# Attention scores on one core: whole head pairs on 128 columns, 16 KB output runs and two-bank transposed tiles

## The chip, the cores and the metric

The kernel runs on one core of a Trainium2 chip. The metric is the device time of one execution in microseconds (us). Engines are called as in the profile: PE is TensorE (matmuls and transposes), DVE is VectorE, ACT is ScalarE, POOL is GpSimd, SP is SyncE, which issues all DMAs here.

## The reference

```
q, k : (8, 8, 512, 64) float32        # batch, heads, sequence, head dimension
scale = 1 / sqrt(64)
out[b, h] = scale * q[b, h] @ k[b, h].T        # (8, 8, 512, 512) float32
```

The inputs are 16.78 MB together and the output is 67.11 MB.

## The kernel before

The work is cut into four units (`v`) of two batches each, and each unit into four output tiles (`t`) of 4 MB: sixteen stores in all. There are five steps.

**Loads and casts** (`load_and_cast`, lines 78 and 82). At the start SP issues, for each unit, one 2 MB load of k and one of q; each of the 128 partitions takes a run of 16 KB. The float32 data of a unit fill one buffer of the pool `big`. POOL casts them to bf16 (`xb`), four casts per unit. `big` has three buffers, which the output tiles use too, so the load of the fourth unit waits for the casts of the first, and an output tile waits until the data that were in its buffer have been cast or stored.

**Transposes** (`transpose`, lines 107 and 116). PE transposes 128x128 blocks of k and q against an identity into a PSUM tile `tp` of eight blocks, one bank. The pool of `tp` has two buffers. A unit has eight such tiles, four for k and four for q.

**Copies** (`rearrange`, line 95). Four copies bring each `tp` to SBUF in another order: to `kT`, or to `qz`, which keeps zeros in the half of its partitions that belongs to the other batch. DVE and ACT take whole tiles in turn (`n_tp % 2`).

**Scores and evacuations** (`scores`, lines 126, 66 and 64). An output tile consists of eight PSUM tiles `ps` of two banks, from a pool of three buffers. Each is filled by four matmuls of 64 columns by 512, two heads on the two column halves, and then scaled and written to the output tile `o` by DVE or ACT: of every six, ACT takes numbers 0, 2 and 3. A partition of `o` holds 16 rows of the output of one head, 32 KB in a row.

**Stores** (line 141). When the eight evacuations are done, SP issues one DMA of 4 MB.

The order of the work is that of the program, held on each engine by `pinned`. The transposes of unit v+1 are a generator, `ahead`, of which `take` draws some steps after each evacuation of unit v. One step is either all transposes of one `tp` or one copy. The first unit is transposed ahead of everything. In unit 0 two steps are drawn per evacuation from the second output tile on:

```
for n, _ in enumerate(scores(v, t)):
    take(ahead, 1 + (n % 4 == 3) if v else 2 * (t > 0))
```

Of the kernel before, what the change touches and what calls it, by code (L numbers as in the profile page):

```python
# [1 line left out]

# [5 lines left out]


@with_exitstack  # L10
def kernel(
    ctx: ExitStack,
    tc: tile.TileContext,
    q: bass.AP,
    k: bass.AP,
    out: bass.AP,
):

    nc = tc.nc
    B, H, S, D = q.shape
    scale = 1.0 / (D ** 0.5)
    P = 128
    UNITS = B // 2
    N = H
    M = P // (2 * H)  # L30
    R = S // M
    J = R // 2
    RO = 16
    U = S // RO
    JJ = J // RO
    IW = 8 // JJ
    TILES = N // 2

    f32 = mybir.dt.float32
    bf16 = mybir.dt.bfloat16  # L40

    q_r = q.rearrange("(v b) g (m j) d -> v (b g m) (j d)", b=2, j=R)
    k_r = k.rearrange("(v b) g (m j) d -> v (b g m) (j d)", b=2, j=R)
    out_r = out.rearrange("(v b) (t h) (u i) k -> v (b t) (h u) (i k)", b=2, h=4, i=RO)

    consts = ctx.enter_context(tc.tile_pool(name="consts", bufs=1))

    big_pool = ctx.enter_context(tc.tile_pool(name="big", bufs=3))
    bf_pool = ctx.enter_context(tc.tile_pool(name="bf", bufs=6))
    t_pool = ctx.enter_context(tc.tile_pool(name="t", bufs=2))  # L50
    tpsum_pool = ctx.enter_context(tc.tile_pool(name="tpsum", bufs=2, space=bass.MemoryType.PSUM))
    psum_pool = ctx.enter_context(tc.tile_pool(name="psum", bufs=3, space=bass.MemoryType.PSUM))


    pinned = tc.keep_in_program_order

    n_evac = 0
    n_tp = 0

    def evacuate(dst, src):  # L60
        nonlocal n_evac

        if n_evac % 6 in (0, 2, 3):
            pinned(nc.scalar.mul(out=dst, in_=src, mul=scale))  # L64
        else:
            pinned(nc.vector.tensor_scalar(out=dst, in0=src, scalar1=scale, scalar2=None,  # L66
                                           op0=mybir.AluOpType.mult))
        n_evac += 1

    def half(h):  # L70
        return slice(h * D, (h + 1) * D)

    def load_and_cast(v):

        xf = big_pool.tile([P, 2, 2, J * D], f32, name="big")
        both = []
        for x, src in enumerate((k_r, q_r)):
            nc.sync.dma_start(out=xf[:, x], in_=src[v].rearrange("p (s c) -> p s c", s=2))
        for x in range(2):
            xb = bf_pool.tile([P, J, 2, D], bf16, name="xb")  # L80
            for s in range(2):
                pinned(nc.gpsimd.tensor_copy(out=xb[:, :, s, :],  # L82
                                             in_=xf[:, x, s].rearrange("p (j d) -> p j d", j=J)))
            both.append(xb)
        return both

    def rearrange(tp, pattern, dst):

        nonlocal n_tp
        copy = (nc.vector.tensor_copy, nc.scalar.copy)[n_tp % 2]  # L90
        n_tp += 1
        for s in range(2):
            src = tp[half(s)].rearrange(pattern, n=N, h=2)
            for h in range(2):
                pinned(copy(out=dst(s, h), in_=src[:, h]))  # L95
                yield

    def transpose(v, kb, qb):


        kT = t_pool.tile([P, N, M, 2, J], bf16, name="kT")
        qz = qzs[v % 2]
        ts[v] = (kT, qz)
        for j0 in range(0, J, 8):
            tp = tpsum_pool.tile([P, 8, P], bf16, name="tp")
            for j in range(8):
                pinned(nc.tensor.transpose(out=tp[:, j, :], identity=identity,  # L107
                                           in_=kb[:, j0 + j].rearrange("p s d -> p (s d)")))
            yield
            yield from rearrange(tp, "d j (n h m) -> d h n m j",  # L110
                                 lambda s, h: kT[half(h), :, :, s, j0:j0 + 8])
        for i0 in range(0, RO, IW):
            tp = tpsum_pool.tile([P, IW, JJ, P], bf16, name="tp")
            for i in range(IW):
                for jj in range(JJ):
                    pinned(nc.tensor.transpose(out=tp[:, i, jj, :], identity=identity,  # L116
                                               in_=qb[:, RO * jj + i0 + i].rearrange("p s d -> p (s d)")))
            yield
            yield from rearrange(tp, "d i jj (n h m) -> d h i n m jj",
                                 lambda s, h: qz[half(h), i0:i0 + IW, :, h * U:(h + 1) * U]  # L120
                                 .rearrange("d i n (m s jj) -> d s i n m jj", s=2, jj=JJ)[:, s])

    def matmul(v, t, i, x, dst):

        kT, qz = ts[v]
        pinned(nc.tensor.matmul(out=dst, lhsT=qz[:, i, 2 * t + x, :],  # L126
                                rhs=kT[:, 2 * t + x].rearrange("d m s j -> d (m s j)"),
                                start=True, stop=True))

    def scores(v, t):  # L130

        o = big_pool.tile([P, RO, S], f32, name="big")
        for i in range(0, RO, 2):
            ps = psum_pool.tile([P, 2, S], f32, name="ps")
            for w in range(2):
                for x in range(2):
                    matmul(v, t, i + w, x, ps[half(x), w, :])
            evacuate(o[:, i:i + 2, :], ps)
            yield
        src = o.rearrange("p i k -> p (i k)")  # L140
        nc.sync.dma_start(out=out_r[v, t], in_=src)  # L141

    def take(steps, count):
        for _ in range(count):
            next(steps, None)

    identity = consts.tile([P, P], dtype=bf16)
    make_identity(nc, identity)
    qzs = [consts.tile([P, RO, N, 2 * U], bf16, name=f"qz{n}") for n in range(2)]
    for qz in qzs:  # L150
        nc.vector.memset(qz, 0.0)  # L151
    cast = [load_and_cast(v) for v in range(UNITS)]

    ts = {}
    for _ in transpose(0, *cast[0]):
        pass
    for v in range(UNITS):
        ahead = transpose(v + 1, *cast[v + 1]) if v + 1 < UNITS else iter(())
        for t in range(TILES):

            for n, _ in enumerate(scores(v, t)):
                take(ahead, 1 + (n % 4 == 3) if v else 2 * (t > 0))
        for _ in ahead:
            pass


# [1 line left out]
_INS = ['q', 'k']  # L168
_OUTS = [((8, 8, 512, 512), 'float32')]


# [23 lines left out]
```

## Time and profile before

| | |
|---|---|
| median of three runs | 203.78 us (203.74 to 204.09) |
| the profiled execution, whole | 203.86 us |
| its span, first to last instruction | 202.1 us |
| PE busy | 107.7 us, 53% of the span |
| DVE busy | 126.4 us, 63% |
| ACT busy | 101.1 us, 50% |
| POOL busy | 30.5 us, 15% |
| DMA: data moved, mean rate | 84.00 MB, 416 GB/s |
| mean granted PE clock | 0.833 |

A line of the groups gives the line of the kernel, the engine, the operation, output and input with their shapes and the count; then the busy time and the mean of one in ns; then the idle time of the engine just before, with what ended it. A line of the timeline gives start and duration in us. The slices cut the span in 40 equal parts: the DMA digit is the busy share of the 16 DMA engines in tenths, 9 meaning 90% or more.

### The profile page before, as it was taken

The page shows a single profiled execution, that of the slowest core. Times are in us where ns is not written, and L with a number is a line of the kernel's source. Part 1 is how long each engine was busy: PE and PEld are TensorE (multiplying, and loading weights), DVE is VectorE, ACT ScalarE, POOL GpSimd, SP SyncE. Part 2 cuts the span into 40 slices and gives each one's busy share as a digit, 9 for nine tenths or more (in the row PEclk, how much of TensorE's full clock was granted, in tenths as well). Part 3 has the DMA queues.
Part 4 walks back from the last instruction along what each step waited for, and adds up shares of the span by engine and source line. Part 5 has one row for each costly group of instructions (what it writes and reads, how often), then busy time and mean ns, then how long its engine had stood idle before and what let it go on. Part 6 is the DMA issues. An engine that isn't in the chain of part 4 may idle for free.

```text
span 202.1 us, 1976 instructions
## 1 busy us (share of the span) xinstructions
PE 107.7 (53%) x768; PEld 55.7 (28%) x768; DVE 126.4 (63%) x130; ACT 101.1 (50%) x129; POOL 30.5 (15%) x22
## 2 busy tenths in 40 slices
PE   0033488663784767765858685856765366710000
PEld 0033344332342333332423332322322133400000
DVE  6736677974987689997569797479457064530000
ACT  2016665793639586974857566746526241520000
POOL 1277777655000000000000000000000000000000
PEclk9999999998769999997878888888589957555555
DMA  6999999999999999999999999999999999999991
GB/s 214 428 444 415 435 441 422 418 412 428 454 438 417 441 417 428 438 448 435 422 415 425 448 435 448 415 418 428 435 448 441 415 428 438 441 428 441 415 415 58
DMA packets 3464, 84.00 MB, mean 416 GB/s; under 512 B 384, under 2 KB 384, under 8 KB 384
## 3 DMA queue, kind: packets, MB, share of 16 engines
q1 hardware_dynamic: 3456, 83.89, 97.2%
q8 instruction: 6, 0.10, 0.2%
q14 instruction: 2, 0.02, 0.0%
HBM read 16.78 MB, written 67.11 MB: 415 GB/s over the span
## 4 chain that ended last, share of the span: by engine, by line
DMA 33%; DVE 14%; PE 6%; ACT 2%; issue 1%; DVEq 0%; ACTq 0%; SPq 0%
DMA out_dram<-big 33%; DVE big L66 9%; PE ps L126 6%; DVE kT L95 3%; ACT big L64 2%; DVE qz L95 1%; ACT kT L95 1%; PE tp L107 0%; DVEq L66 0%; ACTq L64 0%; SPq L141 0%
## 5 line engine op out<-in xcount | busy, mean ns | idle before, releaser
L126 PE MATMUL ps<-kT,qz 128*64 128x512 bf16 x512 | 85.0, 456 | 47.2 <-ACT big L64 36.6
L66 DVE TENSOR_SCALAR big<-ps 128x1024 f32<-128x1024 f32 x64 | 76.2, 1221 | 38.9 <-DMA out_dram<-big 25.0
L64 ACT ACTIVATE big<-ps 128x1024 f32<-128x1024 f32 x64 | 63.9, 1023 | 56.9 <-DMA out_dram<-big 24.5
L126 PEld LDWEIGHTS <-qz 128*64 128x64 bf16 x512 | 35.6, 124 | 85.9 <-issue 75.7
L82 POOL CAST xb<-big 128x2048 bf16<-128x2048 f32 x16 | 29.8, 1893 | 17.1 <-DMA big<-in_k_dram 9.6
L95 DVE COPY kT<-tp 64x512 bf16<-64x512 bf16 x32 | 22.0, 687 | 7.3 <-PE tp L107 6.9
L95 ACT COPY kT<-tp 64x512 bf16<-64x512 bf16 x32 | 18.5, 578 | 15.2 <-PE tp L107 14.9
L95 DVE COPY qz<-tp 64x512 bf16<-64x512 bf16 x32 | 22.0, 688 | 3.9 <-PE tp L116 3.3
L95 ACT COPY qz<-tp 64x512 bf16<-64x512 bf16 x32 | 18.5, 578 | 4.0 <-PE tp L116 3.6
L107 PE MATMUL tp<-identity,xb 128*128 128x128 bf16 x128 | 12.0, 253 | 15.0 <-POOL xb L82 12.4
L116 PE MATMUL tp<-identity,xb 128*128 128x128 bf16 x128 | 13.3, 272 | 7.8 <-ACT qz L95 4.1
L107 PEld LDWEIGHTS <-xb 128*128 128x128 bf16 x128 | 9.5, 114 | 20.8 <-POOL xb L82 12.4
L116 PEld LDWEIGHTS <-xb 128*128 128x128 bf16 x128 | 10.6, 123 | 14.4 <-issue 14.1
L151 DVE MEMSET qz<- 128x4096 uint32 x2 | 6.9, 3472 | 2.5 <-PEq L179 1.7
L95 ACT ACT_TABLE_LOAD x1 | 1.3, 1283 | 0.7 <-PEq L179 0.7
masks.py:199 POOL TENSOR_SCALAR_AFFINE_SELECT identity<-identity 128x128 bf16<-128x128 bf16 x1 | 0.3, 292 | 0.1
masks.py:197 POOL MEMSET identity<- 128x128 bf16 x1 | 0.2, 204 | 0.3 <-POOLq L179 0.3
L179 POOL MEMSET const-float32-0.0<- 128x1 f32 x1 | 0.1, 98 | 0.2 <-issue 0.2
L179 POOL MEMSET const-bfloat16-1.0<- 128x1 bf16 x1 | 0.1, 101 | 0.0
L179 POOL MEMSET const-uint8-127<- 128x1 uint8 x1 | 0.1, 101 | 0.0
L179 POOL MEMSET const-float32-1.0<- 128x1 f32 x1 | 0.1, 98 | 0.0
## 6 DMA issues: line engine op xcount, KB each, us to landing
out_dram<-big SPq DMA_DIRECT2D x16, 4096.0 KB, 21.2
big<-in_k_dram SPq DMA_DIRECT2D x4, 2048.0 KB, 18.9
big<-in_q_dram SPq DMA_DIRECT2D x4, 2048.0 KB, 23.9
```

The lines of the kernel that those rows point to most:

```text
L64: pinned(nc.scalar.mul(out=dst, in_=src, mul=scale))
L66: pinned(nc.vector.tensor_scalar(out=dst, in0=src, scalar1=scale, scalar2=None, op0=mybir.AluOpType.mult))
L82: pinned(nc.gpsimd.tensor_copy(out=xb[:, :, s, :], in_=xf[:, x, s].rearrange("p (j d) -> p j d", j=J)))
L95: pinned(copy(out=dst(s, h), in_=src[:, h]))
L107: pinned(nc.tensor.transpose(out=tp[:, j, :], identity=identity, in_=kb[:, j0 + j].rearrange("p s d -> p (s d)")))
L116: pinned(nc.tensor.transpose(out=tp[:, i, jj, :], identity=identity, in_=qb[:, RO * jj + i0 + i].rearrange("p s d -> p (s d)")))
L126: pinned(nc.tensor.matmul(out=dst, lhsT=qz[:, i, 2 * t + x, :], rhs=kT[:, 2 * t + x].rearrange("d m s j -> d (m s j)"), start=True, stop=T ...
L151: nc.vector.memset(qz, 0.0)
L179: nc = _bacc.Bacc("TRN2", target_bir_lowering=False, num_devices=1)
```

## The change

The head pair `x` moves from the column halves of a matmul to the free dimension of the output tile. A matmul now has 128 columns for one pair of heads, and a `ps` tile takes two matmuls. A partition of `o` holds 8 rows of each of two heads' outputs, two runs of 16 KB that lie 2 MB apart in the output; a store is still 4 MB. A transposed tile has 16 blocks and two banks, and a copy twice the elements; a unit has four such tiles and 16 copies. The pool of `tp` has one buffer, where it had two. The first unit's transposed tiles take their buffers from the pool of `ps` instead. In unit 0 the steps of `ahead` are drawn in the third and fourth output tile alone, one per evacuation and two after every fourth; in later units they are drawn after evacuations 0, 1, 3, 5 and 7, which is one transposed tile with its four copies for each output tile.

```diff
-    RO = 16
+    RO = 8
...
-    IW = 8 // JJ
+    IW = 16 // JJ
...
-    out_r = out.rearrange("(v b) (t h) (u i) k -> v (b t) (h u) (i k)", b=2, h=4, i=RO)
+    out_r = out.rearrange("(v b) (t x h) (u i) k -> v (b t) (h u) x (i k)", b=2, x=2, h=2, i=RO)
...
-    tpsum_pool = ctx.enter_context(tc.tile_pool(name="tpsum", bufs=2, space=bass.MemoryType.PSUM))
+    tpsum_pool = ctx.enter_context(tc.tile_pool(name="tpsum", bufs=1, space=bass.MemoryType.PSUM))
...
-        for j0 in range(0, J, 8):
-            tp = tpsum_pool.tile([P, 8, P], bf16, name="tp")
-            for j in range(8):
+        pool, name = (tpsum_pool, "tp") if v else (psum_pool, "ps")
+        for j0 in range(0, J, 16):
+            tp = pool.tile([P, 16, P], bf16, name=name)
+            for j in range(16):
...
-                                 lambda s, h: kT[half(h), :, :, s, j0:j0 + 8])
+                                 lambda s, h: kT[half(h), :, :, s, j0:j0 + 16])
         for i0 in range(0, RO, IW):
-            tp = tpsum_pool.tile([P, IW, JJ, P], bf16, name="tp")
+            tp = pool.tile([P, IW, JJ, P], bf16, name=name)
...
-    def matmul(v, t, i, x, dst):
+    def scores(v, t):
         kT, qz = ts[v]
-        pinned(nc.tensor.matmul(out=dst, lhsT=qz[:, i, 2 * t + x, :],
-                                rhs=kT[:, 2 * t + x].rearrange("d m s j -> d (m s j)"),
-                                start=True, stop=True))
-    def scores(v, t):
-        o = big_pool.tile([P, RO, S], f32, name="big")
-        for i in range(0, RO, 2):
-            ps = psum_pool.tile([P, 2, S], f32, name="ps")
-            for w in range(2):
-                for x in range(2):
-                    matmul(v, t, i + w, x, ps[half(x), w, :])
-            evacuate(o[:, i:i + 2, :], ps)
-            yield
-        src = o.rearrange("p i k -> p (i k)")
-        nc.sync.dma_start(out=out_r[v, t], in_=src)
+        o = big_pool.tile([P, 2, RO, S], f32, name="big")
+        for x in range(2):
+            n = 2 * t + x
+            for i in range(0, RO, 2):
+                ps = psum_pool.tile([P, 2, S], f32, name="ps")
+                for w in range(2):
+                    pinned(nc.tensor.matmul(out=ps[:, w, :], lhsT=qz[:, i + w, n, :],
+                                            rhs=kT[:, n].rearrange("d m s j -> d (m s j)"),
+                                            start=True, stop=True))
+                evacuate(o[:, x, i:i + 2, :], ps)
+                yield
+        nc.sync.dma_start(out=out_r[v, t], in_=o.rearrange("p x i k -> p x (i k)"))
...
-    qzs = [consts.tile([P, RO, N, 2 * U], bf16, name=f"qz{n}") for n in range(2)]
+    qzs = [consts.tile([P, RO, N, P], bf16, name=f"qz{n}") for n in range(2)]
...
-                take(ahead, 1 + (n % 4 == 3) if v else 2 * (t > 0))
+                take(ahead, (1 + (n % 4 == 3)) * (t > 1) if v == 0 else n == 0 or n % 2)
```

## The prediction

> **What bounds the kernel now.** I read the slices first, then the groups, the timeline around the end of the loads, and the sync queue's issues. The slices show sixteen DMA engines that never rest:
>
> ```profile
> DMA  6999999999999999999999999999999999999991
> GB/s 214 428 444 415 435 441 422 418 412 428 454 438 417 441 417 428 438 448 435 422 415 425 448 435 448 415 418 428 435 448 441 415 428 438 441 428 441 415 415 58
> ...
> q1 hardware_dynamic: 3456, 83.89, 97.2%
> ```
>
> The transfers (83.89 MB) are the bound: at some 431 GB/s they take 194.6 us of the 202.1 us span. What is left is about 1.9 us of start (in the window 0 to 5 us the DMA share is 0.63, so data flows from 5 - 3.15 = 1.85 us, 1.1 us after the first issue) and a tail in which the engines end one by one: the landing marks of the last store run from 196.9 to 200.8 us. So this kernel can gain almost nothing, and it loses exactly what it makes the DMA wait. The question is how far ahead of the DMA the compute engines stay. The groups give the prices:
>
> ```profile
> L66 DVE TENSOR_SCALAR big<-ps 128x1024 f32<-128x1024 f32 x64 | 76.2, 1221 | 38.9 <-DMA out_dram<-big 25.0
> L64 ACT ACTIVATE big<-ps 128x1024 f32<-128x1024 f32 x64 | 63.9, 1023 | 56.9 <-DMA out_dram<-big 24.5
> L95 DVE COPY kT<-tp 64x512 bf16<-64x512 bf16 x32 | 22.0, 687 | 7.3 <-PE tp L107 6.9
> L95 ACT COPY kT<-tp 64x512 bf16<-64x512 bf16 x32 | 18.5, 578 | 15.2 <-PE tp L107 14.9
> ```
>
> And the timeline of 44.2 to 58 us shows where the lead is smallest:
>
> ```profile
> 44.49 3.73 POOL L82 CAST xb<-big 128x2048 bf16<-128x2048 f32 x2 [2.15 <-DMA big<-in_q_dram]
> ...
> 48.25 2.36 DVE L66 TENSOR_SCALAR big<-ps 128x1024 f32<-128x1024 f32 x2 [3.92 <-POOL xb L82]
> ...
> 51.13 1.03 PE L116 MATMUL tp<-identity,xb 128*128 128x128 bf16 x8
> ```
>
> The sync queue's timeline from 50 to 70 us has the next two stores, in one line (first issue, and the time to the end of the second):
>
> ```profile
> 56.91 9.59 SPq L141 DMA_DIRECT2D out_dram<-big  x2
> ```
>
> The third output tile (t=2 of unit 0) reuses the buffer of the last load, so its evacuations cannot begin before 48.25 us, when GpSimd has cast that load. It is issued at 56.91; the store before it lands, engine by engine, from 61.3 to 63.3 us. That is a lead of 4.4 us, and the next are no larger by much: the records of issue are 56.9, 66.2, 74.9, 83.7, 91.1 us, against first landings of the store before at 61.3, 71.0, 80.7, 90.4, 100.0. In the window 56 to 91 us DVE is busy 30.69 of 35 us, with the DMA share at 1.00. An engine that is 88% busy is not far below the bound.
>
> [...]
>
> **The change part by part.**
>
> *Full 128-column matmuls.* 512 matmuls become 256, but the 64-column ones ran in pairs, so a 2-bank tile takes the same time, some 0.65 us with its latency (four matmuls: 0.62). Nothing gained on the path; PE's instruction stream gets shorter.
>
> *16 KB runs.* Stores go from 2048 packets of 32 KB to 4096 of 16 KB. The loads are 16 KB already: 433 GB/s in 5 to 15 us, against about 431 for the stores from 100 to 180 us, so no cost is seen; the packet records (611 ns for 16 KB, 1215 for 32 KB) put it at 2048 x 3.5 ns / 16, about 0.5 us, if every one counts. Writes in two runs 2 MB apart are not shown before: I bound that between -0.5 and +3 us, and take +0.3, since only stores at the DMA's own pace pay it.
>
> *Two-bank transposed tiles, copies of 1024.* 64 + 64 copies of 512 become 32 + 32 of 1024. [...] Total copying falls from 81.0 to 32 x 1.22 + 32 x 1.02 = 71.7 us. But the pool has one buffer, not two: sixteen transposes (T) wait until all four copies of the tile before are done, and the matmuls behind them in PE's order wait too. DVE's copies and ACT's copies no longer overlap.
>
> *Unit 0's own transposes* use the three score buffers. They end before the first buffer is free for output (second load cast at about 27 us), and the first store is needed only at about 42 us: no cost, covered by 7 us or more.
>
> *Unit 1's transposes move* from t=1, 2, 3 (two steps per evacuation) to t=2, 3 alone. The order of the built program in t=2 is: evacuations (e) D D A D A A D D (D on DVE, A on ACT), T0 after the first matmul, four DVE copies among e1 to e3, T1 before the sixth matmul. Walking the queues from 48.25 us: DVE does e0, e1, two copies, e3, two copies = 7 x 1.22 = 8.5, to 56.8. T1 then has its buffer: 2.05 us at the granted clock of this stage (twice the 1.03 of the row at 51.13; PEclk 0.66 to 0.72), to 58.9. The sixth and seventh matmul pairs, 1.6 us; e6 and e7, 2.44. The third store is issued at 63.0, and data flows 1.1 us later, at 64.1. Store 1 ran dry at 61.3: **2.8 us lost** for the engines that were first.
>
> In t=3 (A D A A D D A D): ACT's four copies of T1 run from 60.9 to 65.0; T2 1.25; a matmul pair 0.65; e1 1.22; four DVE copies 4.9; T3 1.25; a pair 0.65; e5, e7 2.44: issue at 77.4. Data at 78.5, against store 2's end at 64.1 + 9.7 = 73.8: **4.7 us lost**. Both tiles work without a reserve, all three buffers being free by then.
>
> Units 1 and 2 carry one T and four copies per tile (eight tiles, 4 to 11). After T come, on the copying engine, four copies and about four evacuations: 8 x 1.22 = 9.8 on DVE tiles, 8 x 1.02 = 8.2 on ACT tiles; with T at 1.2 to 1.5 and some 0.3 for the pair after it, the mean is 9.0 + 1.5 = 10.5 us, against 9.7 for a store. Eight tiles lose 8 x 0.8 = **6.4 us**. Unit 3 has no transposes: four evacuations per engine, 5 to 6 us, so it waits for the DMA again, and nothing is won back.
>
> Walked in the same way, from its own rows, the kernel before gives issues at 57.2, 66.0, 74.5, 83.3 against the recorded 56.9, 66.2, 74.9, 83.7. So the method holds where I can test it.
>
> *What comes off.* When the DMA runs dry the engines start level again, so of the 3.9 us between first and last landing I expect some 2 at the end: -2. Of six instruction fetches (q8, 16 KB) a third falls away; one at 35.2 us delays an engine that brings the last load (43.97 us, when the median engine is done at 42.2). If it falls later, t=2 starts up to 1.3 us earlier: I take -0.6.
>
> Sum on the profiled execution's 203.86 us (span 202.1 and 1.76 around it): 203.86 + 2.8 + 4.7 + 6.4 + 0.3 - 2.0 - 0.6 = 215.5; the median of the runs, 203.78, is the same within 0.1. I say **215.5 us**. With the hand-over times between engines (semaphore, last matmul to first read) at the low end of what before allows, 0.2 us, the same walk loses 11 us of DMA time, at the high end, 0.4 us, 17; the restart after each gap may cost up to 0.5 us (the first packets at the start took 0.8 us rather than 0.61). That makes 211 to 221.
>
> **The rivals.**
>
> *The DMA stays fed* (10%). If copies with 16 long inner runs cost much less than 1.22 us, say 0.8, a DVE tile falls to 4 x 0.8 + 4 x 1.22 + 1.5 = 9.6 and the lead holds in units 1 and 2. It decides at a mean tile of 9.7 us. For it: fewer, longer copies. Against it: 512-element copies cost the same with inner runs of 8 (kT) and of 2 (qz), 687 and 688 ns. What remains is the shorter instruction stream (up to -1) and the packets (+0.5): 203.0 to 204.5; faster by over 0.2% is about half of this case.
>
> *Only the move of unit 1's transposes hurts* (22%). Tile periods of units 1 and 2 come out at 9.7 or below, and the loss is the two gaps of t=2 and 3, 7.5 us, less 2.6: about 209.
>
> *The stores themselves get slower* (8%), by the two runs 2 MB apart: 3% of 155 us of stores, 4.7 us. Alone about 208; on top of the gaps it hides in them in part, 219.
>
> *The forecast* (60%).
>
> **How the numbers follow.** The change of 0.2% (0.4 us) is what a measurement can tell. Slower by more than that: 0.60 + 0.22 + 0.08 and a little of the first rival, 0.91. Within: 0.04. Faster: 0.05. The range takes in the second rival: 208 to 221.
>
> **What would show it.** The DMA slices should fall to 7 or 8 around 61 to 64 and 73 to 79 us and show 9 and 8 mixed up to about 165 us, then 9 to the end. The third and fourth stores should be issued near 63 and 77 us, the next eight 10 to 11 apart. PE's transposes should wait for copies (tp after kT and qz) for tens of us, and DVE and ACT for PE, no longer for the stores. Copies of 1024 should stand at 1.2 and 1.0 us. I am wrong if the DMA share stays at 1.00 from 56 to 165 us, if the copies are well below 1.2 us, or if stores take longer than 9.8 us with data at hand.

## The result, and the profile after

The changed kernel takes 219.28 us in the median (218.88 to 219.86 in four runs) against 203.85 for the kernel before in the four runs beside it (203.78 in the table above): ratio 1.0757, 95% interval 1.0731 to 1.0784. It is slower by 15.4 us, in the range and of the sign that was forecast; the forecast of +11.7 us was too small by a quarter. The profiled execution took 218.88 us with a span of 217.1.

The slices and the DMA queue, from the page of the changed kernel:

```profile
DVE  6639473409447737982966289269768837360000
...
DMA  7999999999969559899979894999999999999994
GB/s 229 429 432 423 432 429 426 417 432 435 432 266 401 232 214 411 341 432 405 420 296 435 338 435 208 423 432 408 417 435 386 435 429 435 401 423 435 435 435 199
...
q1 hardware_dynamic: 5504, 83.89, 91.5%
```

A slice is 5.4 us. The same 83.89 MB now keep the DMA engines busy for 91.5% of a longer span. The holes are where the forecast put them, only deeper (6, 5 and 5 where it had 7 or 8): slice 12 (60 to 65 us), slices 14 and 15 (71 to 81), then single slices up to 136 us, and in the rate once more at 163 to 168 us (386 GB/s); there are none after that. The DMA got work too late. At its work it became only a little slower, 9.72 us a store against 9.68, as the landings below show.

The groups of the changed kernel:

```profile
L66 DVE TENSOR_SCALAR big<-ps 128x1024 f32<-128x1024 f32 x64 | 76.1, 1221 | 58.0 <-PE ps L134 29.9
...
L64 ACT ACTIVATE big<-ps 128x1024 f32<-128x1024 f32 x64 | 63.6, 1023 | 62.0 <-PE ps L134 40.7
...
L95 DVE COPY kT<-tp 64x1024 bf16<-64x1024 bf16 x12 | 14.6, 1220 | 4.5 <-PE tp L109 4.3
L95 ACT COPY qz<-tp 64x1024 bf16<-64x1024 bf16 x12 | 12.1, 1005 | 9.8 <-PE tp L118 9.6
```

The copies of 1024 elements cost 1220 and 1005 ns, close to the evacuations of that length in the kernel before (1221 and 1023 ns), from which they had been priced, and total copying fell (DVE busy 126.4 to 121.7 us). Still, what DVE and ACT wait for ahead of the evacuations has changed from the stores to PE. What PE waits for stands in the waits by engine (us in total, times, the longest):

```profile
PE tp L109 <- DVE kT L95: 11.5, 3, 5.5
...
PE tp L118 <- DVE qz L95: 10.7, 3, 4.3
...
PE tp L109 <- ACT qz L95: 5.9, 2, 3.0
PE tp L118 <- ACT kT L95: 5.4, 3, 2.5
```

Together these are 33.5 us in which PE, at the head of a transposed tile, waits for the copies of the one before. In the kernel before the same waits came to 10.2 us, over 32 tiles instead of 12:

```profile
PE tp L116 <- ACT qz L95: 4.1, 2, 2.4
...
PE tp L107 <- ACT kT L95: 2.4, 1, 2.4
PE tp L116 <- DVE kT L95: 2.1, 1, 2.1
...
PE tp L116 <- ACT kT L95: 1.6, 1, 1.6
```

In the changed kernel the matmuls behind a waiting tile in PE's queue wait too, and the evacuations for them. The timeline from 44 to 80 us shows one round of it (left out: the weight loads, PEld, and the stretches marked by dots):

```profile
48.39 2.36 DVE L66 TENSOR_SCALAR big<-ps 128x1024 f32<-128x1024 f32 x2 [6.52 <-POOL xb L82]
...
54.35 2.47 DVE L95 COPY kT<-tp 64x1024 bf16<-64x1024 bf16 x2
56.87 1.86 PE L109 MATMUL tp<-identity,xb 128*128 128x128 bf16 x16 [5.54 <-DVE kT L95]
58.53 3.62 PE L134 MATMUL ps<-kT,qz 128*128 128x512 bf16 x8
59.63 1.02 ACT L64 ACTIVATE big<-ps 128x1024 f32<-128x1024 f32 x1 [7.24 <-PE ps L134]
60.48 2.36 DVE L66 TENSOR_SCALAR big<-ps 128x1024 f32<-128x1024 f32 x2 [3.66 <-PE ps L134]
60.55 4.05 ACT L95 COPY kT<-tp 64x1024 bf16<-64x1024 bf16 x4
...
64.65 1.11 PE L118 MATMUL tp<-identity,xb 128*128 128x128 bf16 x16 [2.50 <-ACT kT L95]
```

Copies end at 56.82 and the transposes begin at 56.87; ACT's copies end at 64.60, the next begin at 64.65. All eleven tiles of transposes that follow another in the `tp` pool start 0.05 us after that one's last copy. ACT had done nothing for 7.24 us when its evacuation at 59.63 began. The third store was issued at 62.90 us (63.0 forecast), the fourth at 77.99 (77.4).

Each store leaves one landing mark per DMA engine in the trace, a packet of 4 bytes that ends the engine's share (384 for the 24 loads and stores). From the first mark of one store to the first of the next it takes 9.72 us in the changed kernel when nothing is late (51.58 to 61.30); before it took 9.68. The third store lands 12.31 us after the second, the fourth 15.08 after the third; the next eight take 86.47 us, 10.8 each; the last four 9.82 each.

### The profile page after: what moved, and what is told of

Same layout as the page of the kernel before. It is cut to its first block, busy times and chain, and to the rows that moved or that the text cites. A ratio compares the mean times of both kernels' runs of the same rounds, so it can differ in the third digit from the quotient of the medians.

```text
span 217.1 us, 1397 instructions
## 1 busy us (share of the span) xinstructions
PE 111.3 (51%) x512; PEld 52.7 (24%) x512; DVE 121.7 (56%) x98; ACT 96.8 (45%) x97; POOL 30.6 (14%) x22
## 3 DMA queue, kind: packets, MB, share of 16 engines
q1 hardware_dynamic: 5504, 83.89, 91.5%
## 5 line engine op out<-in xcount | busy, mean ns | idle before, releaser
L66 DVE TENSOR_SCALAR big<-ps 128x1024 f32<-128x1024 f32 x64 | 76.1, 1221 | 58.0 <-PE ps L134 29.9
L134 PE MATMUL ps<-kT,qz 128*128 128x512 bf16 x256 | 87.9, 482 | 33.1 <-ACT big L64 23.1
L64 ACT ACTIVATE big<-ps 128x1024 f32<-128x1024 f32 x64 | 63.6, 1023 | 62.0 <-PE ps L134 40.7
L134 PEld LDWEIGHTS <-qz 128*128 128x128 bf16 x256 | 29.6, 118 | 85.2 <-issue 72.1
L82 POOL CAST xb<-big 128x2048 bf16<-128x2048 f32 x16 | 29.9, 1896 | 17.2 <-DMA big<-in_k_dram 10.8
L109 PE MATMUL tp<-identity,xb 128*128 128x128 bf16 x96 | 9.0, 267 | 17.4 <-DVE kT L95 11.5
L118 PE MATMUL tp<-identity,xb 128*128 128x128 bf16 x96 | 9.5, 278 | 16.0 <-DVE qz L95 10.7
L95 DVE COPY kT<-tp 64x1024 bf16<-64x1024 bf16 x12 | 14.6, 1220 | 4.5 <-PE tp L109 4.3
L95 ACT COPY qz<-tp 64x1024 bf16<-64x1024 bf16 x12 | 12.1, 1005 | 9.8 <-PE tp L118 9.6
L95 DVE COPY qz<-tp 64x1024 bf16<-64x1024 bf16 x12 | 14.6, 1220 | 2.2 <-PE tp L118 2.0
L95 ACT COPY kT<-tp 64x1024 bf16<-64x1024 bf16 x12 | 12.1, 1006 | 7.7 <-PE tp L109 7.6
L109 PE MATMUL ps<-identity,xb 128*128 128x128 bf16 x32 | 3.6, 313 | 12.3 <-POOL xb L82 12.3
L95 DVE COPY kT<-ps 64x1024 bf16<-64x1024 bf16 x4 | 4.9, 1222 | 4.9 <-PE ps L109 4.8
L95 DVE COPY qz<-ps 64x1024 bf16<-64x1024 bf16 x4 | 4.9, 1222 | 0.1
L118 PE MATMUL ps<-identity,xb 128*128 128x128 bf16 x32 | 3.8, 310 | 2.3 <-POOL xb L82 1.3
```

The source lines that it names most:

```text
L82: pinned(nc.gpsimd.tensor_copy(out=xb[:, :, s, :], in_=xf[:, x, s].rearrange("p (j d) -> p j d", j=J)))
L134: pinned(nc.tensor.matmul(out=ps[:, w, :], lhsT=qz[:, i + w, n, :], rhs=kT[:, n].rearrange("d m s j -> d (m s j)"), start=True, stop=True))
```

## The experiments

Three theories. **A**: the single buffer of transposed tiles makes transposes and copies follow each other, so a tile takes longer than its store. **B**: moving unit 1's transposes to the last two tiles of unit 0 takes the reserve away. **C**: stores in two 16 KB runs are slow. A diff is against the changed kernel where it does not say otherwise; lines such as `tpsum bufs=1` sum up edits and are not code. The lead of a store, below, is the time from its issue to the first landing of the store before it. In the changed kernel a store that is issued with no store ahead of it lands 10.7 us later (62.90 to 73.61), about 1 us more than its 9.72, so a lead under 1 us already costs time.

### The rest of the change alone

```diff
 # against the changed kernel
-tpsum bufs=1, tiles of 16 blocks, IW = 16 // JJ, first unit in the pool of ps
+tpsum bufs=2, tiles of 8 blocks, IW = 8 // JJ, all units in tpsum
-    take(ahead, (1 + (n % 4 == 3)) * (t > 1) if v == 0 else n == 0 or n % 2)
+    take(ahead, 1 + (n % 4 == 3) if v else 2 * (t > 0))
```

> Full 128-column matmuls and 16 KB stores alone; the transposed tiles, their two buffers and their place in the program are as before. Theory A (one buffer of transposed tiles serializes transposes and copies) and theory B (unit 1's transposes in the last two tiles leave no reserve) both say: no gaps in the DMA, 203 to 205 us, the stores 9.7 to 9.8 us each (0.05 to 0.15 longer than before), fewer instruction fetches. Theory C (stores in two 16 KB runs are slow or restart badly, and cause most of the loss): 210 us or more.

Measured: 203.02 us (202.96 to 203.06), ratio to before 0.9959, interval 0.9944 to 0.9974. The DMA has no hole, and the smallest lead is 4.9 us:

```profile
DMA  6999999999999999999999999999999999999993
```

From first landing to first landing stores take 9.72 us up to 158 us and 9.76 to 9.83 afterwards. C falls: the matmuls of 128 columns and the two-run stores together are slightly *better* than what they replace. On PE's path nothing was gained: at the granted clock of 1.0 a score tile takes 0.59 us with two matmuls of 128 columns in the changed kernel, and 0.62 us with four of 64 in the kernel before, where two start within 0.03 us of each other. The gain is in the tail: the last store's landings spread over 2.26 us instead of 3.90, and these 1.6 us are more than the 0.9 us by which the longer stores delay its first landing (197.74 against 196.85 us).

### One-bank tiles in two buffers, the rest as changed

```diff
-tpsum bufs=1, tiles of 16 blocks, IW = 16 // JJ, first unit in the pool of ps
+tpsum bufs=2, tiles of 8 blocks, IW = 8 // JJ, all units in tpsum
-    take(ahead, (1 + (n % 4 == 3)) * (t > 1) if v == 0 else n == 0 or n % 2)
+    take(ahead, 2 * (1 + (n % 4 == 3)) * (t > 1) if v == 0 else 2 * (n == 0 or n % 2))
```

> The change with one-bank transposed tiles in two buffers put back; unit 1 is still transposed in its last two tiles. A: the 8.7 us that units 1 and 2 lose go, and of the 8.0 us lost in unit 0 about half, since DVE's 5 evacuations and 8 copies of 0.69 us (11.6 us) still exceed 9.7: 205 to 209 us. B: the 8 us of unit 0 stay whole, 211 us or more. C: no change from 219.

Measured: 203.41 us (203.10 to 203.84), ratio 0.9979, interval 0.9971 to 0.9987. All of the loss is gone, though unit 1 is still transposed in the last two tiles: the third store is issued at 58.94 us, the fourth at 69.15, both in time, though with leads of 2.3 and 1.8 us only. I had expected some 2 to 4 us of loss in unit 0 to stay; with two buffers there is none, and the time lies below the 205 to 209 us that A expected.

### Two-bank tiles in two buffers

```diff
-tpsum bufs=1, psum bufs=3
+tpsum bufs=2, psum bufs=2
```

> The change with two buffers of two-bank transposed tiles; the score tiles get two buffers instead of three to make room. A: transposes no longer wait for the copies of the tile just before, DVE's and ACT's copies overlap; tile periods of units 1 and 2 fall below 9.7 us, the loss of unit 0 halves: 206 to 212 us, unless two score buffers cost as much as they give. B: 8 us of unit 0 stay, 211 us or more. C: 219.

Measured: 203.42 us (202.93 to 205.22), ratio 0.9997, interval 0.9979 to 1.0014. The ratio cannot be told from 1; A had expected 206 to 212 us, so here too more came back than it said. This keeps the size of the tiles, the copies and the place; only the second buffer is back, paid for with a score buffer. The tile view of `tp` lists what ended the idle time before the instructions on these tiles. For this kernel its list is complete with two entries, and there is no wait of PE for copies in place of the 33.5 us:

```profile
its engine sat idle before it (us, times) until:
  PE tp L109: 2.1, 3
  PE tp L118: 1.8, 3
who waited for it (us, times):
```

and its slices are full:

```profile
DMA  6999999999999999999999999999999999999995
```

So the two-bank size and the long copies are harmless in the median, and the number of buffers decides. The reserve is small, though: the fourth to seventh stores have leads of 0.5 to 1.0 us, and the sixth, issued 0.5 us ahead of need, lands 0.5 us late. Seven of the 20 executions took 204.4 to 205.2 us.

### Unit 1's steps from the second tile on, single buffer kept

```diff
-    take(ahead, (1 + (n % 4 == 3)) * (t > 1) if v == 0 else n == 0 or n % 2)
+    take(ahead, (t > 0) if v == 0 else n == 0 or n % 2)
```

> The change with unit 1's steps drawn from the second tile on (one per evacuation over three tiles), single two-bank buffer kept. A: unit 0 loses nothing and enters unit 1 with a reserve of a few us; units 1 and 2 still take 10.8 us per tile against 9.7, so most of their 8.7 us less the reserve stays: 207 to 212 us. B: 203 to 205 us. C: no change from 219.

Measured: 209.05 us (208.28 to 209.66), ratio 1.0253, interval 1.0226 to 1.0281. With a single buffer the place is worth 10.2 us (219.28 - 209.05), and 6.0 us over the rest alone remain, as A said. In one point A was wrong: unit 0 does lose, its third store comes 2.3 us late.

```profile
DMA  6999999999988999999999969999999999999994
```

The slices are fed for most of the span, with a dent at 57 to 67 us, where the third store is late, and one at 119 to 124.

### The place alone, in the kernel before

```diff
 # against the kernel before
-    take(ahead, 1 + (n % 4 == 3) if v else 2 * (t > 0))
+    take(ahead, 1 + (n % 4 == 3) if v else (2 + n % 2) * (t > 1))
```

> The kernel before with nothing changed but the place of unit 1's transposes: all forty steps in the third and fourth output tile of unit 0 (two or three per evacuation), one-bank tiles in two buffers. Theory A (the single buffer is the cause, the move alone costs nothing that the lead does not cover): 203.4 to 204.5 us, the third store issued near 59 us, no gap. Theory B (the move alone takes the reserve): the third and fourth store late by 8 us together, 209 us or more.

Measured: 204.02 us (203.83 to 204.27), ratio 1.0011, interval 1.0002 to 1.0019. The move uses up the reserve almost exactly: the third store is issued at 60.73 us instead of 56.91, and it and the next land 0.4 and 0.6 us late. Less than that reaches the end: 0.24 us in the median. B alone falls; the place costs much only together with the single buffer.

### One buffer alone, in the kernel before

```diff
 # against the kernel before
-tpsum bufs=2
+tpsum bufs=1
```

> The kernel before with one buffer for its one-bank transposed tiles, nothing else. A: transposes wait for the four copies of the tile before, DVE's and ACT's copies no longer overlap, a tile with two transposed tiles takes 2 x 0.65 + 4 x 0.69 + 4 x 0.58 for these and some 5 for evacuations in their way, about 10 to 11 us against 9.7: 206 to 212 us. B and C (stores): 203.8.

Measured: 239.47 us (238.61 to 240.05), ratio 1.1744, interval 1.1715 to 1.1773, far more than expected. The slices, and the tile view of `tp`:

```profile
DMA  7999999096966949892999294899596898999994
```

```profile
its engine sat idle before it (us, times) until:
  PE tp L107: 40.0, 9
  PE tp L116: 31.2, 11
  DVE kT L95: 21.1, 8
  DVE qz L95: 20.7, 8
```

PE waits for DVE's copies alone 41.8 us. A store of units 1 and 2 takes 12.4 us from issue to issue (86.25 to 185.80 us for eight), where I had 10 to 11. My sum took eight copies in a row and forgot that with tiles half as large there are twice as many hand-overs in each output tile. It also left out the first unit, whose transposes are now serial: the first store is issued at 47.5 us instead of 35.0, after the loads have ended, and lands 6.5 us later. The changed kernel loses less with its single buffer (10.8 us for such a store). That this is due to its larger tiles is likely, but no version that differs in this alone was run.

### The four copies shared between DVE and ACT

```diff
-        copy = (nc.vector.tensor_copy, nc.scalar.copy)[n_tp % 2]
         n_tp += 1
         for s in range(2):
+            copy = (nc.vector.tensor_copy, nc.scalar.copy)[s]
```

> The change with each transposed tile's four copies shared, two on DVE and two on ACT, still one two-bank buffer and unit 1 in the last two tiles. A: a tile's copies last 2.4 us on the longer side instead of 4.9, the chain per tile falls to 1.5 + 2 x 1.22 + 4 x 1.22 = 8.8 us, below 9.7, and the DMA is fed: 203 to 206 us, the third store issued near 60 us instead of 63. B: unit 0 still loses most of its 8 us, 209 us or more.

Measured: 214.40 us (213.24 to 214.67), ratio 1.0507, interval 1.0477 to 1.0536: a miss for A. Unit 0 keeps its loss, as B said. The timeline from 44 to 80 us says why (weight loads left out):

```profile
50.02 2.44 DVE L95 COPY kT<-tp 64x1024 bf16<-64x1024 bf16 x2
52.48 1.23 DVE L66 TENSOR_SCALAR big<-ps 128x1024 f32<-128x1024 f32 x1
52.49 2.03 ACT L95 COPY kT<-tp 64x1024 bf16<-64x1024 bf16 x2 [3.72 <-DVE kT L95]
54.54 1.02 ACT L64 ACTIVATE big<-ps 128x1024 f32<-128x1024 f32 x1
54.56 1.86 PE L109 MATMUL tp<-identity,xb 128*128 128x128 bf16 x16 [4.72 <-ACT kT L95]
```

ACT's two copies wait for DVE's two (52.49, after 3.72 us of idling for `DVE kT`), although they read and write other partitions: the built program orders the two engines' work on one tile. Most likely it is the tile that they read: in the kernel before DVE and ACT write one `kT` at the same time out of two `tp` tiles (13.48 to 16.27 us and 14.33 to 16.68). The four copies take 4.5 us, about as in the changed kernel (4.9 on DVE, 4.1 on ACT), not 2.4. The kernel still loses some 8 us in the last two tiles of unit 0 (stores issued at 61.95 and 78.14), while units 1 and 2 lose little after the first two tiles of unit 1, probably because neither engine carries four copies in one tile.

### The same, from the second tile on

The edit of the last experiment (`e6_split` in the expectation) and that of the fourth together.

> As e6_split, and unit 1's steps drawn from the second tile on, one per evacuation. A and B both: no gap at all, 202.5 to 203.5 us; if the single buffer still stalls somewhere, 204 or more. A candidate for the fastest version, with fewer instructions than any other that is fed.

Measured: 203.04 us (202.89 to 203.23), ratio 0.9961, interval 0.9946 to 0.9975. Even the single buffer is enough when its copies are shared and the work of unit 1 is spread over three tiles; the smallest lead is 2.1 us. With the first experiment it is the fastest version found: both beat the kernel before by 0.4% and cannot be told apart.

### Size of the runs alone, in the kernel before

```diff
 # against the kernel before: a gap of 64 bytes in each half of the SBUF tile keeps the runs apart
-        o = big_pool.tile([P, RO, S], f32, name="big")
+        o = big_pool.tile([P, 2, RO // 2 * S + 16], f32, name="big")
...
-        nc.sync.dma_start(out=out_r[v, t], in_=src)
+        nc.sync.dma_start(out=out_r[v, t].rearrange("p (s c) -> p s c", s=2), in_=o[:, :, :8 * S])
```

The tile of the loads, which shares the buffers, and the slice that an evacuation writes are fitted to the gap.

> The kernel before with its stores cut into two 16 KB runs per partition, which still lie side by side in the output (the SBUF tile has a gap of 64 bytes in each half, so the runs cannot be joined); nothing else. If the size of the runs makes the stores of the change slower (9.72 us from landing to landing against 9.68), the stores here take 9.72 too and the kernel 204.2 to 204.6 us. If it is their lying 2 MB apart: 9.68 and 203.8.

Measured: 204.11 us (203.95 to 204.30), ratio 1.0016, interval 1.0009 to 1.0023. Stores take 9.72 us from first landing to first landing (90.55 to 100.27), as in the changed kernel when nothing is late. So the 0.04 us more per store is the size of the runs. But here it stays 9.72 to the end, where the first experiment has up to 9.83 after 158 us. Whether the 2 MB between the runs have a part in that is open.

### Two buffers of two-bank tiles, from the second tile on

The edits of the third and fourth experiment together.

> The change with two buffers of two-bank transposed tiles, two score buffers, and unit 1's steps from the second output tile on. Theory A (the buffer count decides): no gap, 202.8 to 203.4 us, as the other fed versions; two score buffers cost nothing that the DMA sees. If two score buffers are too few, 204 or more.

Measured: 203.89 us, but spread from 202.88 to 204.51; ratio 0.9998, interval 0.9984 to 1.0012. The median misses the 202.8 to 203.4 us of A, and ten of the 22 executions took over 204 us, the mark set for too few score buffers. The profiled one, 203.65 us, has no hole in the DMA, but its smallest lead is 1.3 us, against 4.9 in the first experiment. Both versions with two score buffers spread in this way (17 of 42 executions over 204 us); of the three fed versions with one-bank tiles or shared copies and three score buffers, none of 23 took more than 203.84. So giving a score buffer for the second transposed tile goes with about 1 us more in part of the executions. None of the slow ones was traced, and why they are slow is open.

## Why the prediction was right, and where its sum was short

The medians, by the two parts that matter:

| unit 1's transposes | two buffers of `tp` | one buffer of `tp` |
|---|---|---|
| from the second tile on | 203.02 (one-bank), 203.89 (two-bank) | 209.05 |
| last two tiles only | 203.41 (one-bank), 203.42 (two-bank) | 219.28 |

The mechanism was the forecast one. With two buffers neither place loses more than 0.4 us; with one both do. Together the two causes cost more than each alone, 16.3 us against 6.0 and 0.4, because the move leaves no reserve for the slower tiles to draw on. The rival in which only unit 1's move hurts is refuted: alone it costs 0.24 us, and units 1 and 2 did lose. So is the rival of slow stores, by the first experiment; that it named 219 us for stores on top of the gaps, nearer to the result than my 215.5, is chance. The rival in which the DMA stays fed would have needed cheap copies; they cost 1.22 us. That the engines keep to the order of their queues, on which the walk rests, shows in the trace: PE's score matmuls of 58.53 us start behind the transposes that had waited until 56.87. DVE stands idle until 66.70 us for an evacuation, with copies behind it whose transposes had ended at 65.76, and ACT 0.70 us until 139.03, with three copies of its tile still to do.

Step by step, in us:

| term of the sum | forecast | measured |
|---|---|---|
| third store late | 2.8 | 2.6 (12.31 - 9.72) |
| fourth store late | 4.7 | 5.4 (15.08 - 9.72) |
| units 1 and 2, eight tiles | 6.4 | 8.7 (86.47 - 8 x 9.72) |
| 16 KB stores | 0.3 | 1.0 (15 x 0.04, and 4 x 0.10 at the end) |
| engines level at the end | -2.0 | -2.4 (spread 3.90 to 1.46) |
| fetches that fall away before the last load | -0.6 | 0.0 (last load lands at 44.04, before 43.97) |
| sum | 11.6 | 15.3; the span grew by 15.0 |

The term that was mis-sized most is that of units 1 and 2, though the single tile was sized right. I took 1.5 us from the first transpose to the first copy and 9.0 for the copies with the evacuations between them. Over the eight tiles the trace has 2.3 and 8.1 on average. The second is less because some evacuations lie outside; the first is more because sixteen transposes take 1.05 to 1.11 us where the granted clock is 1.0 and 1.86 where it is 0.5 (as in the windows 145.2 to 146.2 and 135.4 to 137.3 us), and because in three of the eight tiles an evacuation stands in front of the first copy (3.3 to 3.9 us). With the 0.05 us of hand-over the sum is 10.5 us, as forecast. That is luck in part, since one half was too small by about what the other was too large. From the first transposes of this stage at 80.32 us to its last copy at 164.29 us the chain has no gap, 84.0 us for eight. But the eight stores came 86.4 us apart from issue to issue (77.99 to 164.42), 10.8 each. Of the 2.4 us between, 2.3 lie ahead of the chain:

```profile
77.22 3.04 ACT L95 COPY qz<-tp 64x1024 bf16<-64x1024 bf16 x3
77.99 0.37 SPq L139 DMA_DIRECT2D out_dram<-big  x1
...
80.32 1.86 PE L109 MATMUL tp<-identity,xb 128*128 128x128 bf16 x16 [2.88 <-ACT qz L95]
```

When the fourth store was issued, ACT still had copies of unit 1's last transposed tile to do, until 80.27 us, and the next transposes waited for them. The sum had no place for this. Single tiles differ much, 8.1 to 12.4 us from issue to issue and five of the eight 11 or more, where the forecast had 10 to 11; but the stores at both ends of the stage came late, so the loss of the stage follows from the length of the chain and what lies ahead of it.

The fourth store was later than walked because T3 took 1.87 us, not 1.25: in the window 72.8 to 74.7 us the granted clock is 0.50. In 50 to 61 us it is 0.50 too (before, 48 to 61: 0.74); there the forecast had taken the low clock, with 2.05 us for T1, and 1.86 came of it. The fetch that delays an engine ahead of the last load did fall later, at 41.8 us instead of 35.2, but still before that load had ended: the landings of the load before it spread over 0.6 us, those of the last over 2.2. So nothing came of it.

Two smaller steps of the prediction do not hold. By its own figures the leads do not stay near 4.4 us: they grow to 8.9 (91.1 to 100.0). And its packet records give twice the price for 16 KB runs: 2 x 611 - 1215 = 7 ns for each of 2048 pairs, over 16 engines, is 0.9 us and not 0.5; the undisturbed stores cost 0.6 and the slower ones at the end 0.4 more. One of its signs of being wrong did show: with data at hand the last four stores take 9.82 us each, just over the limit of 9.8. That is 0.4 us in all and stands in the row of the 16 KB stores; it does not touch the cause.

## What to carry to other kernels

A DMA queue that never rests did not show here how near it was to running dry (between the first slice and the last all are nines with a smallest lead of 4.9 us, in the rest alone, and of 0.5, with two-bank tiles in two buffers): find by how much each transfer is issued ahead of its need, stage by stage, and price a change against that lead and not against busy shares. The pool of one buffer turned a producer and its consumers into one chain (84.0 us for eight tiles, without a gap), and what stood behind the producer in its queue joined it: with unit 1 in the last two tiles the second buffer was worth 16 us, while in two buffers the tile's size and the longer copies cost nothing in the median. Look at the lead of the pool that gives up the room as well: with two score buffers instead of three the median was the same (203.42 and 203.41 us), but the smallest lead fell from 1.8 to 0.5 us and a third of the executions took at least 1 us more than that median.

## What the hardware showed that I had not expected

- In the changed kernel the stores of most engines take 9.82 us, not 9.72, after a gap or late in the run, when the engines run nearly level (all 16 landings of one store lie between 164.82 and 164.97 us), while an engine that lags keeps 9.72. In the version with the rest of the change alone the first landings of the last two stores are 9.80 us apart, the last landings 9.72 (190.28 to 200.00). Small runs are not needed for it: with 32 KB runs, in the kernel before with the place moved, first landings are 9.72 to 9.74 us apart once the late third and fourth stores have brought most engines level, and most last landings 9.68. That the engines disturb each other when they run level is a guess; it was not tried.
- In the kernel before, one DMA engine loses 0.15 to 0.3 us per store between 107 and 180 us, by the last landings, while the compute engines work, and ends 1.9 us after all others. In the version with the rest of the change alone, with 512 fewer PE instructions of matmul and weight load, it loses at most 0.2 and the end comes 0.8 us earlier. Between these two versions the loss shrinks with the instructions; the cause was not isolated.
